# Combining two expert outputs per token: three rooms of 16 tokens, token-wise products, and paired stores

## The chip, the core and the metric

The kernel runs on one core of a Trainium2 chip. The metric is the device time of one execution in microseconds; smaller is better. Before the change the median of three runs is 239.19 us (239.14 to 239.21).

## The reference

There are 16 x 1024 = 16,384 tokens. Each has two expert outputs of 512 float32 numbers and two weights, and the result is their weighted sum:

```python
# expert_outputs (16, 1024, 2, 512), combine_weights (16, 1024, 2), float32
weights = combine_weights[..., np.newaxis]
return np.sum(expert_outputs * weights, axis=2).astype(np.float32)   # (16, 1024, 512)
```

A token brings 4 KB in and 2 KB out. All tokens together bring 67.1 MB in, 33.6 MB out, and 0.13 MB of weights. Nothing is reused.

## The kernel before

The tokens are spread over the 128 partitions, 128 tokens to a partition. In the first region of the tensors each partition owns 120 consecutive tokens, in the second one 8, so that a tile's tokens are one unbroken run of memory in each partition. A tile of 12 tokens is thus loaded as 128 rows of 48 KB and stored as 128 rows of 24 KB. There are ten tiles of 12 tokens and a last one of 8. Tile 0 is loaded in two parts, first 2 tokens (in rows of 4 KB) and then 10.

The loop over the tiles (line 68) takes a buffer from a pool of four (`ipool`, `bufs=4`, 48 KB per partition each, 192 KB in all), issues the load on SP's queue (line 75), computes in place, and issues the store from the same buffer. The results are packed into the lower half of the buffer, `ot`. The load of tile g + 4 needs the buffer of tile g, so on SP it waits until the store of tile g has landed.

For tiles 0 to 8, VectorE (DVE in the profile) does everything in two large instructions: line 84 multiplies both halves of 12 tokens by their weights (128 x 12,288 elements), and line 85 adds the halves (128 x 6,144). ScalarE (ACT) only issues the stores (line 86). For the last two tiles ACT multiplies the first half of each token by its weight (line 92), token after token. For tile 9 DVE multiplies the second half (line 107) and adds (line 108); for the last tile DVE does both for one token in one instruction, `scalar_tensor_tensor`: second half times weight plus first half (line 96). The stores of these two tiles are issued on SP (line 109), behind all loads.

Ahead of the loop, DVE clears a small tile `zt`, which ACT's queue writes to the start of 16 stretches of the output (line 58; the real results overwrite it later); then the weights `wt` are loaded on ACT's queue in two parts (line 62), and a one-element activation (line 66) brings in ACT's table. A tile scheduler sets the order on each engine; within one queue it is as in the text, but for the store of tile 8, which stands between the eighth and the ninth activation of tile 9.

SP and ACT each have one DMA queue. Both are served by the same 16 DMA engines; each engine moves 8 of the 128 rows of a transfer. In the page "q1" is SP's queue and "q10" is ACT's.

Of the kernel before, what the change touches and what calls it, by code (L numbers as in the profile page):

```python
# [1 line left out]

# [4 lines left out]


@with_exitstack
def kernel(  # L10
    ctx: ExitStack,
    tc: tile.TileContext,
    expert_outputs: bass.AP,
    combine_weights: bass.AP,
    out: bass.AP,
):

    nc = tc.nc  # L20
    b, s, k, h = expert_outputs.shape
    assert k == 2
    n = b * s
    P = nc.NUM_PARTITIONS
    per = n // P
    assert per * P == n
    J, LAST = 12, 8
    main = per - LAST
    assert main % J == 0
    eo = expert_outputs.rearrange("b s k h -> (b s) (k h)")  # L30
    cw = combine_weights.rearrange("b s k -> (b s) k")
    o = out.rearrange("b s h -> (b s) h")

    def rows(x):

        a = x[0 : P * main, :].rearrange("(p t) f -> p t f", p=P)
        b = x[P * main : n, :].rearrange("(p t) f -> p t f", p=P)
        return lambda t, c: a[:, t : t + c, :] if t < main else b[:, t - main : t - main + c, :]

    eo, cw, o = rows(eo), rows(cw), rows(o)  # L40

    dt = mybir.dt.float32
    mult = mybir.AluOpType.mult
    add = mybir.AluOpType.add
    copy = mybir.ActivationFunctionType.Copy

    last = main // J

    wpool = ctx.enter_context(tc.tile_pool(name="w", bufs=1))
    ipool = ctx.enter_context(tc.tile_pool(name="in", bufs=4))  # L50

    wt = wpool.tile([P, per * k], dt)


    zt = wpool.tile([16, 128], dt)
    nc.vector.memset(zt, 0.0)  # L56
    first = out.rearrange("b s h -> (b s) h")[0 : P * main, :].rearrange("(q t) h -> q (t h)", q=16)
    ahead = nc.scalar.dma_start(out=first[:, 0:128], in_=zt)  # L58

    with tc.issue_after(ahead.ins):  # L60
        for t, c in ((0, main), (main, LAST)):
            nc.scalar.dma_start(
                out=wt[:, k * t : k * (t + c)].rearrange("p (t k) -> p t k", k=k), in_=cw(t, c)
            )
        warm = wpool.tile([P, 1], dt)
        nc.scalar.activation(out=warm, in_=nc.const_aps.tensor(1.0, (P, 1), dt), func=copy)  # L66

    for g in range(last + 1):
        et = ipool.tile([P, J, k * h], dt)

        ot = et.rearrange("p j f -> p (j f)")[:, 0 : J * h].rearrange("p (j f) -> p j f", f=h)
        t0, c = g * J, J if g < last else LAST

        for a, m in ((0, 2), (2, c - 2)) if g == 0 else ((0, c),):
            nc.sync.dma_start(  # L75
                out=et[:, a : a + m],
                in_=eo(t0 + a, m),
                max_dma_last_dim=k * h * 4 if g + a == 0 else None,
            )
        if g < last - 1:  # L80

            wb = wt[:, g * J * k : (g + 1) * J * k].unsqueeze(2).to_broadcast([P, J * k, h])
            ek = et.rearrange("p j (k h) -> p (j k) h", k=k)
            nc.vector.tensor_tensor(out=ek, in0=ek, in1=wb, op=mult)  # L84
            nc.vector.tensor_tensor(out=ot, in0=et[:, :, 0:h], in1=et[:, :, h : 2 * h], op=add)  # L85
            nc.scalar.dma_start(out=o(t0, c), in_=ot)
            continue


        for i in range(c):  # L90
            t = t0 + i
            nc.scalar.activation(  # L92
                out=et[:, i, 0:h], in_=et[:, i, 0:h], func=copy, scale=wt[:, 2 * t : 2 * t + 1]
            )
            if g == last:
                nc.vector.scalar_tensor_tensor(  # L96
                    out=ot[:, i, :],
                    in0=et[:, i, h : 2 * h],
                    scalar=wt[:, 2 * t + 1 : 2 * t + 2],
                    in1=et[:, i, 0:h],  # L100
                    op0=mult,
                    op1=add,
                )
        if g < last:
            w1 = wt.rearrange("p (t k) -> p t k", k=k)[:, t0 : t0 + c, 1:2]
            x1 = et[:, :, h : 2 * h]
            nc.vector.tensor_tensor(out=x1, in0=x1, in1=w1.to_broadcast([P, c, h]), op=mult)  # L107
            nc.vector.tensor_tensor(out=ot, in0=et[:, :, 0:h], in1=x1, op=add)  # L108
        nc.sync.dma_start(out=o(t0, c), in_=ot[:, 0:c])


# [1 line left out]
_INS = ['expert_outputs', 'combine_weights']  # L113
_OUTS = [((16, 1024, 512), 'float32')]


# [23 lines left out]
```

## Time and profile before

| | before |
|---|---|
| median of three runs | 239.19 us |
| span of the profiled execution | 237.34 us |
| DMA traffic | 100.80 MB in 3,760 packets |
| DVE busy | 194.1 us, 29 instructions |
| ACT busy | 14.0 us, 22 instructions |
| TensorE, GpSimd | no work of the kernel |

The profiled execution has no separately listed time of its own; the span covers the work from the first to the last instruction on the core, and the runs without a profile take 239.19 us, 1.85 us more than the span. The clock of TensorE plays no part, as it has no work.

How to read the page: "busy" is the time in which an engine executed an instruction. A DMA packet here is one row of a transfer (or a 4-byte write that raises a semaphore at its end; 16 for each DMA). "Idle before, releaser" says how long the engine waited ahead of a group of instructions and what ended the longest part of the wait. "Queue's own waits" of SP are the waits of the engine that only issues DMAs.

### The profile page before, as it was taken

The numbers are of one execution on the slowest core, as the hardware profiler recorded it, in microseconds if no ns is written. First come the engines' busy times: TensorE is split into PE (matmuls) and PEld (weight loads), VectorE is DVE, ScalarE is ACT, GpSimd is POOL, SyncE is SP. The second block draws the span as 40 slices with busy tenths as digits, with TensorE's granted clock in tenths as the row PEclk, the third lists the DMA queues.
The fourth block names the chain that finished last, engine by engine and source line by source line (L and its number), as shares of the span: only waits on it lengthen the run. The fifth ranks groups of instructions, "written<-read, shape, count | busy, mean of one in ns | idle before, by whom it ended". The sixth has DMA issues, their size and how long they took to land.

```text
span 237.3 us, 157 instructions
## 1 busy us (share of the span) xinstructions
DVE 194.1 (82%) x29; ACT 14.0 (6%) x22; POOL 0.2 (0%) x4
## 2 busy tenths in 40 slices
DVE  0008999999999999999999889969996998785710
ACT  2000000000000000000000000000000000740800
POOL 0000000000000000000000000000000000000000
DMA  7999999989899999999898999999998979999997
GB/s 289 452 474 398 398 448 480 398 356 505 352 443 435 427 464 464 398 398 530 348 514 348 447 418 443 464 464 398 398 522 348 522 344 451 464 398 442 406 434 309
DMA packets 3760, 100.80 MB, mean 425 GB/s; under 512 B 544, under 2 KB 688, under 8 KB 944
## 3 DMA queue, kind: packets, MB, share of 16 engines
q1 hardware_dynamic: 2144, 72.35, 71.0%
q10 hardware_dynamic: 1616, 28.45, 27.9%
HBM read 67.24 MB, written 33.56 MB: 425 GB/s over the span
## 4 chain that ended last, share of the span: by engine, by line
DMA 59%; DVE 34%; ACT 2%; ACTq 0%; DVEq 0%; issue 0%; SPq 0%
DMA out_dram<-et 29%; DMA et<-in_expert_outputs_dram 23%; DVE et L84 22%; DVE et L85 11%; DMA wt<-in_combine_weights_dram 7%; ACT et L92 2%; DVE et L96 1%; DVEq L135 0%; ACTq L135 0%; ACTq L58 0%; DVE zt L56 0%; DVEq L84 0%; SPq L75 0%; ACTq L92 0%
## 5 line engine op out<-in xcount | busy, mean ns | idle before, releaser
L84 DVE TENSOR_TENSOR et<-et,wt 128x12288 f32<-128x12288 f32 x9 | 116.6, 12955 | 24.1 <-DMA wt<-in_combine_weights_dram 17.5
L85 DVE TENSOR_TENSOR et<-et 128x6144 f32<-128x6144 f32 x9 | 59.0, 6557 | 0.3
L92 ACT ACTIVATE et<-et,wt 128x512 f32<-128x512 f32 x20 | 12.5, 708 | 208.6 <-DMA et<-in_expert_outputs_dram 208.6
L96 DVE SCALAR_TENSOR_TENSOR et<-et,wt 128x512 f32<-128x512 f32 x8 | 5.6, 746 | 3.9 <-ACT et L92 3.6
L107 DVE TENSOR_TENSOR et<-et,wt 128x6144 f32<-128x6144 f32 x1 | 6.6, 6557 | 2.3 <-DMA et<-in_expert_outputs_dram 2.3
L108 DVE TENSOR_TENSOR et<-et 128x6144 f32<-128x6144 f32 x1 | 6.6, 6558 | 0.9 <-ACT et L92 0.9
L66 ACT ACT_TABLE_LOAD x1 | 1.3, 1283 | 2.4 <-issue 2.4
L56 DVE MEMSET zt<- 16x128 f32 x1 | 0.2, 165 | 0.8 <-PEq L124 0.8
L66 ACT ACTIVATE warm<-const-float32-1.0 128x1 f32<-128x1 f32 x1 | 0.2, 202 | 0.0
L124 POOL MEMSET const-bfloat16-1.0<- 128x1 bf16 x1 | 0.1, 102 | 0.0
L124 POOL MEMSET const-uint8-127<- 128x1 uint8 x1 | 0.1, 101 | 0.0
L124 POOL MEMSET const-float32-0.0<- 128x1 f32 x1 | 0.1, 99 | 0.2 <-issue 0.2
L124 POOL MEMSET const-float32-1.0<- 128x1 f32 x1 | 0.1, 98 | 0.0
## 6 DMA issues: line engine op xcount, KB each, us to landing
et<-in_expert_outputs_dram SPq DMA_DIRECT2D x9, 6144.0 KB, 29.9
out_dram<-et ACTq DMA_DIRECT2D x9, 3072.0 KB, 33.0
et<-in_expert_outputs_dram SPq DMA_DIRECT2D x1, 5120.0 KB, 17.0
et<-in_expert_outputs_dram SPq DMA_DIRECT2D x1, 4096.0 KB, 25.1
out_dram<-et SPq DMA_DIRECT2D x1, 3072.0 KB, 14.6
out_dram<-et SPq DMA_DIRECT2D x1, 2048.0 KB, 10.0
et<-in_expert_outputs_dram SPq DMA_DIRECT2D x1, 1024.0 KB, 5.0
wt<-in_combine_weights_dram ACTq DMA_DIRECT2D x1, 120.0 KB, 17.0
```

What stands on the lines that cost most here:

```text
L56: nc.vector.memset(zt, 0.0)
L66: nc.scalar.activation(out=warm, in_=nc.const_aps.tensor(1.0, (P, 1), dt), func=copy)
L84: nc.vector.tensor_tensor(out=ek, in0=ek, in1=wb, op=mult)
L85: nc.vector.tensor_tensor(out=ot, in0=et[:, :, 0:h], in1=et[:, :, h : 2 * h], op=add)
L92: nc.scalar.activation(out=et[:, i, 0:h], in_=et[:, i, 0:h], func=copy, scale=wt[:, 2 * t : 2 * t + 1])
L96: nc.vector.scalar_tensor_tensor(out=ot[:, i, :], in0=et[:, i, h : 2 * h], scalar=wt[:, 2 * t + 1 : 2 * t + 2], in1=et[:, i, 0:h], op0=mul ...
L107: nc.vector.tensor_tensor(out=x1, in0=x1, in1=w1.to_broadcast([P, c, h]), op=mult)
L108: nc.vector.tensor_tensor(out=ot, in0=et[:, :, 0:h], in1=x1, op=add)
L124: nc = _bacc.Bacc("TRN2", target_bir_lowering=False, num_devices=1)
```

## The change

The loop and the pool are replaced by a fixed program in which every instruction is placed by hand (`tc.manual_schedule()`: the order on each engine is the order of the text).

- **Regions.** The first region gives each partition 116 tokens, the second 12.
- **Rooms.** One tile `et` of 48 tokens per partition (192 KB) is divided into three rooms of 16 tokens side by side. Tile g lives in room g modulo 3.
- **Tiles.** Nine tiles of 12, 16, 16, 16, 16, 16, 16, 8 and 12 tokens. Loads are rows of 64 KB (16 tokens), 48 KB (12) and 32 KB (8); tile 0 still comes as 2 and 10 tokens.
- **Products.** `combine` treats every token the way the last tile was treated before: one activation on ACT (line 76) and one `scalar_tensor_tensor` on DVE (line 77). These are 128 instructions on each engine. On DVE the 20 large instructions are gone.
- **Stores.** Seven stores instead of eleven. Tiles 3 and 4 (rooms 0 and 1) and tiles 6 and 7 (rooms 0 and 1) are stored together: the earlier tile packs its results into the upper half of its room (`up`, from its last token backwards), the later one into the lower half of the next room, so that both lie side by side and leave as one row of 64 KB (32 tokens) or 48 KB (24 tokens). The other stores are rows of 24 KB (tile 0, tile 8) and 32 KB (tiles 1, 2, 5).
- **Queues.** Loads on SP. The first five stores are issued on ACT, the last two (tiles 6 and 7; tile 8) on SP. The load of tile g + 3 is issued after the store that holds tile g has landed; for tiles 6 and 7 this is the common store of tiles 3 and 4. On SP the order is: loads 0 to 8, store of tiles 6 and 7, store of tile 8.

```diff
-    J, LAST = 12, 8
-    main = per - LAST
...
+    ROOM, ROOMS = 16, 3
+    TILES = [12, 16, 16, 16, 16, 16, 16, 8, 12]
+    STORES = [[0], [1], [2], [3, 4], [5], [6, 7], [8]]
+    AHEAD = 2
+    main = per - TILES[-1]
+    starts = [sum(TILES[:g]) for g in range(len(TILES))]
...
-    ipool = ctx.enter_context(tc.tile_pool(name="in", bufs=4))
+    et = pool.tile([P, ROOMS * ROOM, k * h], dt)
+    halves = et.rearrange("p j (k h) -> p (j k) h", k=k)
...
+    def load(g):
+        at, c = g % ROOMS * ROOM, TILES[g]
+        for a, m in ((0, AHEAD), (AHEAD, c - AHEAD)) if g == 0 else ((0, c),):
+            nc.sync.dma_start(
+                out=et[:, at + a : at + a + m],
+                in_=eo(starts[g] + a, m),
+                max_dma_last_dim=k * h * 4 if g + a == 0 else None,
+            )
+    def combine(g, up):
+        at, c = g % ROOMS * ROOM, TILES[g]
+        base = k * at + (ROOM if up else 0)
+        for i in range(c - 1, -1, -1) if up else range(c):
+            t = k * (starts[g] + i)
+            x0, x1 = halves[:, k * (at + i), :], halves[:, k * (at + i) + 1, :]
+            nc.scalar.activation(out=x0, in_=x0, func=copy, scale=wt[:, t : t + 1])
+            nc.vector.scalar_tensor_tensor(
+                out=halves[:, base + i, :], in0=x1, scalar=wt[:, t + 1 : t + 2], in1=x0, op0=mult, op1=add
+            )
+        return base
+    with tc.manual_schedule():
...
+        for g in range(ROOMS):
+            load(g)
+        for j, st in enumerate(STORES):
+            bases = [combine(g, up=len(st) == 2 and g == st[0]) for g in st]
+            c = sum(TILES[g] for g in st)
+            q = nc.sync if j >= len(STORES) - 2 else nc.scalar
+            q.dma_start(out=o(starts[st[0]], c), in_=halves[:, bases[0] : bases[0] + c, :])
+            for g in st:
+                if g + ROOMS < len(TILES):
+                    load(g + ROOMS)
...
-    for g in range(last + 1):
-        et = ipool.tile([P, J, k * h], dt)
...
-        if g < last - 1:
-            wb = wt[:, g * J * k : (g + 1) * J * k].unsqueeze(2).to_broadcast([P, J * k, h])
-            nc.vector.tensor_tensor(out=ek, in0=ek, in1=wb, op=mult)
-            nc.vector.tensor_tensor(out=ot, in0=et[:, :, 0:h], in1=et[:, :, h : 2 * h], op=add)
-            nc.scalar.dma_start(out=o(t0, c), in_=ot)
```

The line numbers 64, 76, 77 and 100 of the kernel after are its loads, its activations, its DVE instructions and its stores.

More of the change, by code (lines that the diff above doesn't have):

```diff
@@ L26 @@
     assert per * P == n
-    J, LAST = 12, 8
-    main = per - LAST
[L29 to L32, printed above, removed]
-    def rows(x):
[L36 to L40, printed above, removed]
+    ROOM, ROOMS = 16, 3
+    TILES = [12, 16, 16, 16, 16, 16, 16, 8, 12]
+    STORES = [[0], [1], [2], [3, 4], [5], [6, 7], [8]]
+    AHEAD = 2
+    assert sum(TILES) == per and [g for st in STORES for g in st] == list(range(len(TILES)))
+    main = per - TILES[-1]
+    starts = [sum(TILES[:g]) for g in range(len(TILES))]
+    def rows(x):
+        first = x[0 : P * main, :].rearrange("(p t) f -> p t f", p=P)
+        second = x[P * main : n, :].rearrange("(p t) f -> p t f", p=P)
+        return lambda t, c: first[:, t : t + c, :] if t < main else second[:, t - main : t - main + c, :]
+    flat = out.rearrange("b s h -> (b s) h")
+    eo = rows(expert_outputs.rearrange("b s k h -> (b s) (k h)"))
+    cw = rows(combine_weights.rearrange("b s k -> (b s) k"))
+    o = rows(flat)
     dt = mybir.dt.float32
@@ L45 @@
     copy = mybir.ActivationFunctionType.Copy
-    last = main // J
-    wpool = ctx.enter_context(tc.tile_pool(name="w", bufs=1))
-    ipool = ctx.enter_context(tc.tile_pool(name="in", bufs=4))
[L52 to L61, printed above, removed]
+    pool = ctx.enter_context(tc.tile_pool(name="all", bufs=1))
+    et = pool.tile([P, ROOMS * ROOM, k * h], dt)
+    halves = et.rearrange("p j (k h) -> p (j k) h", k=k)
+    wt = pool.tile([P, per * k], dt)
+    zt = pool.tile([16, 128], dt)
+    warm = pool.tile([P, 1], dt)
+    def load(g):
[18 more added lines that the diff above has]
+    with tc.manual_schedule():
+        nc.vector.memset(zt, 0.0)
+        ahead = flat[0 : P * main, :].rearrange("(q t) h -> q (t h)", q=16)
+        nc.scalar.dma_start(out=ahead[:, 0:128], in_=zt)
+        for t, c in ((0, main), (main, per - main)):
             nc.scalar.dma_start(
@@ L64 @@
             )
-        warm = wpool.tile([P, 1], dt)
         nc.scalar.activation(out=warm, in_=nc.const_aps.tensor(1.0, (P, 1), dt), func=copy)
-    for g in range(last + 1):
-        et = ipool.tile([P, J, k * h], dt)
[L71 to L79, printed above, removed]
-        if g < last - 1:
-            wb = wt[:, g * J * k : (g + 1) * J * k].unsqueeze(2).to_broadcast([P, J * k, h])
-            ek = et.rearrange("p j (k h) -> p (j k) h", k=k)
-            nc.vector.tensor_tensor(out=ek, in0=ek, in1=wb, op=mult)
-            nc.vector.tensor_tensor(out=ot, in0=et[:, :, 0:h], in1=et[:, :, h : 2 * h], op=add)
-            nc.scalar.dma_start(out=o(t0, c), in_=ot)
[L87 to L109, printed above, removed]
@@ new lines @@
+        for g in range(ROOMS):
[3 more added lines that the diff above has]
+            c = sum(TILES[g] for g in st)
+            assert bases[-1] == bases[0] + sum(TILES[g] for g in st[:-1])
+            q = nc.sync if j >= len(STORES) - 2 else nc.scalar
[3 more added lines that the diff above has]
+                    load(g + ROOMS)
```

## Prediction

> **What bounds the kernel now.** I read the page's shares first, then its DMA parts, then the DMA share by stretches, then the waits of SP's queue and the chain that ended last.
>
> ```profile
> DVE 194.1 (82%) x29; ACT 14.0 (6%) x22; POOL 0.2 (0%) x4
> ...
> DMA packets 3760, 100.80 MB, mean 425 GB/s; under 512 B 544, under 2 KB 688, under 8 KB 944
> ...
> q1 hardware_dynamic: 2144, 72.35, 71.0%
> q10 hardware_dynamic: 1616, 28.45, 27.9%
> ...
> L84 DVE TENSOR_TENSOR et<-et,wt 128x12288 f32<-128x12288 f32 x9 | 116.6, 12955 | 24.1 <-DMA wt<-in_combine_weights_dram 17.5
> L85 DVE TENSOR_TENSOR et<-et 128x6144 f32<-128x6144 f32 x9 | 59.0, 6557 | 0.3
> L92 ACT ACTIVATE et<-et,wt 128x512 f32<-128x512 f32 x20 | 12.5, 708 | 208.6 <-DMA et<-in_expert_outputs_dram 208.6
> L96 DVE SCALAR_TENSOR_TENSOR et<-et,wt 128x512 f32<-128x512 f32 x8 | 5.6, 746 | 3.9 <-ACT et L92 3.6
> ```
>
> DVE looks like the limit at 82%, but the two queues took 71.0 + 27.9 = 98.9% of the DMA engines' time: 234.7 of 237.3 us. The stretches (their columns: start:end, length, busy time of DVE, ACT and GpSimd, TensorE's clock, DMA share, GB/s) say where the rest is:
>
> ```profile
> 2.00:40.00 38.00, 21.51 (x3) 1.49 (x2) 0.00 (x0) 1.00 1.03 437
> 40.00:120.00 80.00, 79.83 (x9) 0.00 (x0) 0.00 (x0) 1.00 1.00 428
> 120.00:200.00 80.00, 73.28 (x8) 0.00 (x0) 0.00 (x0) 1.00 1.01 437
> ...
> 2.00:236.00 234.00, 193.97 (x28) 13.96 (x22) 0.00 (x0) 1.00 1.00 431
> ```
>
> A packet is credited to the stretch in which it starts, so single stretches stray around 1.00. From 2 to 236 us the share is 1.00: no engine of the 16 ever ran dry. By the packet records the first row starts at 1.8 us and the last ends at 236.1. So 234.3 us is the DMA's own work and 3.0 us its head and tail. The waits of SP's queue and the chain agree:
>
> ```profile
> SPq L75 <- DMA out_dram<-et: 174.1, 7, 45.8
> ```
> ```profile
> 76.96 30.61 DMA out_dram<-et
> 107.57 0.02 SPq L75
> 107.59 0.04 issue
> 107.63 29.93 DMA et<-in_expert_outputs_dram
> 137.56 0.03 issue
> ```
>
> SP waits 174.1 us for stores to free buffers, and the chain goes from store to load to DVE. Yet these waits cost nothing, because other transfers filled the engines meanwhile. DVE's 194 us lie beneath the DMA. The kernel gets faster only through less DMA work, and slower as soon as the queues run dry.
>
> **The bytes, and the packets.** The bytes stay at 100.7 MB plus completion writes. What changes is the number of rows. Median durations in the trace's packet records: 16 KB 611 ns, 24 KB 912, 32 KB 1,213, 40 KB 1,514, 48 KB 1,815, 4-byte completion 9. Every 8 KB costs 301 ns; 9 ns are left over whatever the size. A 64 KB row doesn't occur before; continued, it costs 8 x 301 + 9 = 2,417 ns.
>
> Each engine moves 8 rows of a transfer (16 of the first load's 4 KB rows). Loads before: 16 + 8 + 9 x 8 + 8 = 104 rows; after: 16 + 8 + 6 x 8 + 8 + 8 = 88. Stores before: 11 x 8 = 88; after: 7 x 8 = 56. That is 48 fewer. DMAs go from 26 to 20: 6 fewer completion writes. 54 x 9 ns = 0.49 us saved on each engine, all on the path, since the engines are never idle.
>
> Here the Trainium skill can be weighed. The page "DMA: Bandwidth & Descriptors", section "Anatomy of one DMA", puts about 2.0 us of fixed cost on each DMA; six fewer would by that estimate save 12 us. The share of 1.00 across DMA boundaries says that this cost lies under other transfers. The same page, under "Where 436 GB/s comes from", says that HBM, at about 358 GB/s per core, binds transfers between HBM and SBUF; fewer rows would then gain nothing. Here 431 GB/s passed, so the trace speaks against it.
>
> **The products.** DVE loses 20 large instructions (116.6 + 59.0 us, and 13.1 for lines 107 and 108) and gets 128 of 746 ns; ACT gets 128 of 708 ns. In the last tile eight tokens took 5.78 us on DVE by the timeline, 0.72 each. DVE falls to about 92 us and ACT to 128 x 0.61 = 78. None of this is on the path; it only matters how soon a tile's store is issued: 0.8 us for the first activation plus 16 x 0.72, or 12.3 us (before: 19.5 for 12 tokens). ACT's store stands behind its activations and waits for DVE's last product, and the next tile's activations queue behind it; that tile is usually still loading. Some 200 more instructions must be fetched; the trace has 0.02 to 0.05 us between instructions and no fetch stall, so I take 0, with 0 to 0.6 us as bounds (0.6 is twice the 301 ns of 8 KB on one engine).
>
> **Three rooms instead of four.** This is where time can be lost: a load waits for a store of the tile three back, two tiles share one store, and SP's queue is in order. Behind load 6, which waits for the common store of 3 and 4, stand loads 7 and 8 and both last stores. The rows show how queues share: each engine takes one row from each queue in turn. About 1.1 us pass from issue to first row (0.72 to 1.8), and from a store's last row to the release of SP about 1.6 us (fitted: stepping before's rows through with these two numbers puts loads 4 to 10 at 63.9, 85.8, 107.6 ... 194.8; the trace has 64.1, 85.9, 107.6 ... 194.7).
>
> Counting back from the end, if no gap occurs: the last row ends at 236.1 - 0.5 = 235.6. Store 8 (8 x 0.912) starts at 228.3; store 6+7 (8 x 1.815) at 213.8; load 8 (14.5) at 199.3, which is load 7's end. Load 7 (9.7), load 6 (19.3) and store 5 (9.7) fill 160.6 to 199.3; load 5 and store 3+4 (19.3 each) fill 121.9 to 160.6. Against this, what must be issued in time:
> - Load 5 at about 117 + 1.1 (store 2: eight turns of 2.417 + 1.213 from 86, plus 1.6). Needed at 121.9: cover near 4 us.
> - Store 5: load 5 lands near 144, tile 5 to 156.3, first row 157.4. Needed at 160.6, when store 3+4 runs out and load 6 has not been released: cover 3.2.
> - Store 6+7: load 6 lands at 191.2 (199.3 - 9.7 + 1.6), 12.3 + 0.8 + 5.8 of products to 210.1, first row 211.2. Needed at 213.8: cover 2.6.
> - Store 8: load 8 lands at 215.4, products to 224.8, first row 225.9. Needed at 228.3: cover 2.4.
>
> All four hold, so I price the gaps at 0, with the bound above in the rival. Head and tail stay: load 0 and the weights come as before, and the last store's completion too. One more term: the 48 KB rows that ran between 41 and 47 us, as the first store began, took up to 2.33 us instead of 1.815, together 0.6 us per engine. It happens once, at the first store, which remains; I keep it, with 0 to twice its size as bounds.
>
> **Sum.** 237.34 - 0.49 = 236.85 us of span; with the 1.85 us that lie around it, 238.70 us. With the 0.6 us either way: 238.1 to 239.3. A change below 0.2% (0.48 us) can't be told from none by a measurement of this kernel; the forecast sits just beyond it.
>
> **Rivals.**
> - *The 64 KB rows are split into two of 32 KB.* For: no row above 48 KB occurs in the trace. Against: 48 KB rows go unsplit. Price: 6 x 8 loads and 8 stores more, 56 x 9 ns = 0.50 us, which eats the gain: 239.2.
> - *Queues run dry at the end* (slower). Place: load 8's last row, after which only store 6+7 can follow. It decides at 24 tokens x pace: a cover of 2.6 us is used up when a token takes 0.83 us instead of 0.72. For: the first three DVE products of the last tile started 0.85 us apart; at 0.85 all along, 24 x 0.02 = 0.5 us would be lost: 239.2. At 0.95 it is 2.9 us: 241.6. Against: the later ones started 0.67 apart while transfers ran at full rate. Where it decides I take a pace of 0.88, 240.0.
> - *The first-store stall grows*, or fetching shows: up to 0.6 us on top, 239.3.
>
> **Chances.** Forecast (saving holds, no gap) 65%: it spreads over 238.1 to 239.0 and is beyond the 0.2% in two of three cases (0.43 faster, 0.22 same). Split rows 8%, nearly all within 0.2%. Dry queues 20%, nearly all slower. Stall or fetch 7%, half within 0.2% and half slower. Together: faster 0.44, same 0.32, slower 0.24. The range: 238.2 below; above, it takes in the dry queue up to 240.4, a pace of about 0.90. The likeliest case's own range is 238.1 to 239.0.
>
> **What would show it.** Right: 2,896 packets (16 engines x (88 + 56 + 17 + 20)), 64 KB rows at 2.42 us, DMA share 1.00 from 2 to 235, span near 236.9, DVE near 95 us. Wrong: a stretch with share clearly below 1 near 121, 160, 213 or 228 us (dry queues: read which store came late); more packets than 3,000 (split rows); DVE products further apart than 0.8 us.

## The result, and the profile after

The kernel after takes 242.36 us (median of 4 runs, 242.19 to 242.72) against 239.20 us for the kernel before on the same chip: a ratio of 1.0135, 95% interval 1.0121 to 1.015. It is 3.2 us slower; the forecast was 0.5 us less. Its profiled span is 240.41 us, 3.07 us more than before.

From the page of the kernel after:

```profile
DVE 87.3 (36%) x129; ACT 80.8 (34%) x130; POOL 0.2 (0%) x4
...
DMA packets 2899, 100.83 MB, mean 419 GB/s; under 512 B 448, under 2 KB 592, under 8 KB 848
...
q1 hardware_dynamic: 1856, 76.55, 74.9%
q10 hardware_dynamic: 1040, 24.26, 23.7%
q14 instruction: 3, 0.02, 0.0%
...
L77 DVE SCALAR_TENSOR_TENSOR et<-et,wt 128x512 f32<-128x512 f32 x128 | 87.1, 745 | 138.6 <-ACT et L76 136.8
L76 ACT ACTIVATE et<-et,wt 128x512 f32<-128x512 f32 x128 | 79.3, 707 | 141.8 <-DMA et<-in_expert_outputs_dram 127.5
```

DVE has fallen from 194 to 87 us, and the packets from 3,760 to 2,896 and three that did not exist before: queue 14 fetches instructions during the run. The two data queues still took 98.6% of the engines' time, but of a longer span. So the engines were as busy as before, with fewer rows and the same bytes. They must have worked more slowly somewhere, and the stretches show where (start:end, length, busy DVE, ACT and GpSimd, clock, DMA share, GB/s):

```profile
63.00:66.00 3.00, 0.75 (x1) 1.54 (x3) 0.00 (x0) 1.00 0.89 382
66.00:69.00 3.00, 2.83 (x5) 3.00 (x6) 0.00 (x0) 1.00 1.22 492
69.00:72.00 3.00, 3.00 (x5) 3.00 (x6) 0.00 (x0) 1.00 1.13 350
...
160.00:170.00 10.00, 0.48 (x1) 0.00 (x0) 0.00 (x0) 1.00 0.99 370
165.00:170.00 5.00, 0.00 (x0) 0.00 (x0) 0.00 (x0) 1.00 1.22 413
```

Share and GB/s are both credited to the stretch in which a packet starts, so their quotient is the rate of busy engines, nearly free of that straying. It is 382 / 0.89 = 429 in the first line, and 433 in the undisturbed stretches before. From 66 to 69 it is 403, from 69 to 72 it is 310, from 165 to 170 it is 339. In the last line the engines were busy for 1.22 x 5 = 6.1 us and moved what takes 413 x 5 / 433 = 4.8 us at the full rate: 1.3 us were lost while the share said "full". In the packet records these are a few rows of each engine: usually 1.213 us for 32 KB and 2.418 for 64 KB, near 68 and 167 us up to 2.1 and 3.9 us, on all 16 engines within some 3 us. The chain and SP's waits tell what else happened there:

```profile
SPq L64 <- DMA out_dram<-et: 164.5, 5, 46.6
```
```profile
76.32 40.52 DMA out_dram<-et
116.84 0.02 SPq L64
116.86 0.04 issue
116.90 31.66 DMA et<-in_expert_outputs_dram
...
160.51 24.89 DMA out_dram<-et
185.42 0.03 SPq L64
185.45 0.03 issue
185.47 32.02 DMA et<-in_expert_outputs_dram
```

Load 3 was issued at 64.7 us and load 6 at 163.1 us, each after the load before it had landed (64.4 and 148.6). SP's queue was empty for about 6 us the first time and for about 20 the second, with only stores running. Both slow spots lie where loads begin again. I call this a restart.

The packet records account for the 3.07 us of span. On one engine a row begins 3 to 4 ns before the record of the row ahead of it ends, so a row saved is worth 9 less 3.5, or 5.5 ns. "Excess" is what rows took beyond their usual durations, summed over all rows and divided by 16 engines, apart for the rows that start before and after 6 us; "late" is the end of the last row less that of the eighth last:

| us | before | after | difference |
|---|---|---|---|
| rows and completions saved (54 per engine x 5.5 ns) | | | -0.30 |
| excess before 6 us | 0.57 | 0.41 | -0.16 |
| excess after 6 us | 0.54 | 3.31 | +2.77 |
| late last engine | 0.18 | 0.71 | +0.53 |
| last row's end to the span's end | 1.20 | 1.43 | +0.23 |
| sum | | | +3.07 |

Further down, "the excess" is that after 6 us. This is the account of one execution of each kernel.

### The profile page after: what moved, and what is told of

It is laid out like the page before. It is cut to its first block, busy times and chain, and to the rows that moved or that the text cites. A ratio compares the mean times of both kernels' runs of the same rounds, so it can differ in the third digit from the quotient of the medians.

```text
span 240.4 us, 413 instructions
## 1 busy us (share of the span) xinstructions
DVE 87.3 (36%) x129; ACT 80.8 (34%) x130; POOL 0.2 (0%) x4
## 4 chain that ended last, share of the span: by engine, by line
DMA 69%; DVE 10%; ACT 7%; another core or an unknown queue 6%; issue 1%; ACTq 0%; SPq 0%; DVEq 0%
DMA et<-in_expert_outputs_dram 41%; DMA out_dram<-et 27%; DVE et L77 10%; ACT et L76 7%; SPq L64 0%; DVEq L129 0%; ACTq L129 0%; ACTq L100 0%; ACTq L76 0%
## 5 line engine op out<-in xcount | busy, mean ns | idle before, releaser
L77 DVE SCALAR_TENSOR_TENSOR et<-et,wt 128x512 f32<-128x512 f32 x128 | 87.1, 745 | 138.6 <-ACT et L76 136.8
L76 ACT ACTIVATE et<-et,wt 128x512 f32<-128x512 f32 x128 | 79.3, 707 | 141.8 <-DMA et<-in_expert_outputs_dram 127.5
```

The source lines that it names most:

```text
L76: nc.scalar.activation(out=x0, in_=x0, func=copy, scale=wt[:, t : t + 1])
L77: nc.vector.scalar_tensor_tensor(out=halves[:, base + i, :], in0=x1, scalar=wt[:, t + 1 : t + 2], in1=x0, op0=mult, op1=add)
```

## The experiments

Times are medians, with the ratio to the kernel before measured beside them; rows, stalls and excess are those of the one profiled execution of each run. Theory R (later G): restarts of a queue beside the other cost time. F: instruction fetches in the run. S: 64 KB rows. P: token-wise products.

**e1_solo34: load 6 released by a single store.**

```diff
-    STORES = [[0], [1], [2], [3, 4], [5], [6, 7], [8]]
+    STORES = [[0], [1], [2], [3], [4], [5], [6, 7], [8]]
```

> The changed kernel with tiles 3 and 4 stored each on its own (rows of 32 KB, one more DMA); tiles 6 and 7 stay paired. Theory R (a queue that ran empty and starts again beside the other one stalls the engines' rows: here SP's load queue, empty from 63 to 69 us and from 144 to 168 us in the kernel after, each restart costing about 1.2 us): load 6 is released by store 3 before load 5 ends, the rows near 166 to 170 us go back to 2.42 and 1.21 us, 1.2 us less than after: about 241.1. Rival S (64 KB rows are slower whenever they alternate with stores): nothing moves, 242.4. Rival F (instruction fetches inside the run): nothing moves, 242.4.

241.77 us, ratio 1.011 (1.0097 to 1.0123). The second slow spot is gone:

```profile
165.00:170.00 5.00, 5.00 (x8) 3.18 (x6) 0.00 (x0) 1.00 1.18 511
```

511 / 1.18 = 433, the full rate, with 64 KB and 32 KB rows taking turns. The excess fell from 3.31 to 1.80 us. The median fell by only 0.6 us, not by the 1.2 expected; in the profiled execution one engine ended 1.2 us behind the eighth last (238.23 against 237.03). R is right about the stall; S falls, since 64 KB rows ran beside stores from 75 to 185 us at their usual 2.418 us.

**e2_wt2_sp and e3_both: store 0 freed from the weights.**

```diff
-        for t, c in ((0, main), (main, per - main)):
-            nc.scalar.dma_start(...)
+        def weights(q, t, c):
+            q.dma_start(...)
+        weights(nc.scalar, 0, main)
...
         for g in range(ROOMS):
             load(g)
+        weights(nc.sync, main, per - main)
```

> The changed kernel with the second part of the weights (12 tokens, 8 rows per engine of 96 bytes) loaded on SP's queue after load 2 instead of on ACT's. In the kernel after these rows took turns with 64 KB rows until 36.9 us, and store 0, issued at 27.4, stood behind them. Theory R: store 0 lands some 5 to 8 us earlier, load 3 is released at about 58 to 60 us, near the end of load 2 (63); if it makes it, the stall at 67 to 70 us goes and the time falls by 1.2 us to 241.1; if the queue still runs empty for a moment, the stall stays and 242.4 with it. Rivals S and F: 242.4.

> Both edits, tiles 3 and 4 stored alone and the second part of the weights on SP. Theory R: no restart of the load queue, 2.4 us less than after: 239.9, with 64 KB rows of 2.42 us throughout. Rivals S and F: 242.4.

e2: 242.39 us, 1.0133 (1.012 to 1.0146). e3: 242.3 us, 1.0123 (1.01 to 1.0146), with single runs from 240.76 to 242.73. Store 0 landed at 57.4 instead of 64.6 us, load 3 was issued at 57.5, and the stall at 67 to 70 us disappeared in both. But others came: 0.6 us near 30 and 36 as store 0 began (0.5 before), and 0.5 us near 83 to 85. There it was ACT's queue that had run empty: store 1 landed at about 75, store 2 was issued at 80.2. In e2 the stall at 166 to 169 stayed (1.6 us), in e3 another 0.6 us appeared near 212. The excess was 2.98 and 1.87 us. In e2 a stall was moved, not saved. In e3 the excess is 1.4 us below that of the kernel after, but the last engine ended 1.8 us behind the eighth last (238.97 against 237.15), and the time stayed. The expected 1.2 and 2.4 us did not come.

**e4_12x4: the sizes of before with token-wise products.**

```diff
-    ROOM, ROOMS = 16, 3
-    TILES = [12, 16, 16, 16, 16, 16, 16, 8, 12]
-    STORES = [[0], [1], [2], [3, 4], [5], [6, 7], [8]]
+    ROOM, ROOMS = 12, 4
+    TILES = [12] * 10 + [8]
+    STORES = [[g] for g in range(11)]
```

> The changed kernel's program (token-wise products, manual order) with the sizes of before: four rooms of 12 tokens, tiles of ten times 12 and one of 8, each stored alone, the last two on SP. No 64 KB rows, no pairs, and a load queue that never runs empty. Theory R: as before but for fetches, 239.2 to 239.8. Rival S: 239.2 too. Rival F, or the products themselves being the cause: stays near 242.

242.43 us, 1.0139 (1.0126 to 1.0152). R's 239.2 to 239.8 was missed, but not through stalls: the excess is 0.70 us (0.54 in the kernel before). The time went into idle engines at the end:

```profile
231.00:234.00 3.00, 2.48 (x4) 0.95 (x2) 0.00 (x0) 1.00 0.04 16
```

With quick products the first stores are issued earlier (27.5 us instead of 38.0 for store 0), stores take turns with loads throughout, and push the loads back: the last load was issued at 187.4 us instead of 194.7 and landed at 227.0 instead of 219.8. When its products were under way, no store was left to run. That DVE's slow products held stores back in the kernel before, and that these covered the end, is my reading of the two traces; no run tests it by itself.

**e7_12x4_pair89: the same with a long store under the last products.** `STORES` ends in `[8, 9], [10]`.

> Four rooms of 12 tokens as in e4_12x4, but tiles 8 and 9 stored together on SP (48 KB rows), so that a long store lies under the products of the last tile. The load queue never runs empty, and the gap of about 3 us at 231 to 234 us should close. Theory R: no stall but the one at the first store, and only the fetches remain: 239.3 to 239.9. If the token-wise products or the manual order cost something of their own: above 240.5.

241.69 us, 1.0107 (1.0094 to 1.012). The excess is again 0.70 us, and the gap moved:

```profile
216.00:219.00 3.00, 2.25 (x4) 0.53 (x1) 0.00 (x0) 1.00 0.03 14
```

About 2.5 us of idle engines, as the paired store was issued only at 218.3 us, when the rows of the last load had run out on nearly all engines (it landed at 219.0). Less that gap the time is 239.2. So the expected 239.3 to 239.9 was missed through idle time that I had not seen; in e4 and e7 token-wise products came with no stretched rows beyond those at the first store.

**e5_12x3_pair34: restarts without 64 KB rows.** `ROOM, ROOMS = 12, 3`, tiles as in e4, only tiles 3 and 4 paired.

> The changed kernel's program with rows no longer than 48 KB: three rooms of 12 tokens, ten tiles of 12 and one of 8, only tiles 3 and 4 stored together (48 KB rows). The load queue must run empty before load 3 (three rooms) and before load 6 (waits for the common store). Theory R (restart of an empty queue beside the other): rows around both restarts are stretched, about three quarters of the 1.2 us that 64 KB and 32 KB rows showed, 0.9 us each, so the rows' excess over their usual durations is about 0.6 + 1.8 = 2.4 us per engine. Rival S (only 64 KB rows are slow): excess 0.6 us, as in the kernel before. Both leave the gap of about 3 us at the end that four rooms of 12 showed (231 to 234 us), so 242 under S and 244 under R.

243.40 us, 1.0179 (1.0154 to 1.0205), single runs from 242.37 to 245.3. Rows of 48 and 24 KB stall as well, 1.1 us at the restart of load 6 near 135 us (0.9 expected):

```profile
134.00:137.00 3.00, 0.00 (x0) 0.00 (x0) 0.00 (x0) 1.00 1.26 401
```

401 / 1.26 = 318. There is more at 59 to 70, 111, 163 to 165 and 203 to 206 us. The excess of 3.86 us is above the expected 2.4; it is that of the slowest of the six runs. S is out.

**e6_before_more_instr: instruction fetches alone.**

```diff
         nc.scalar.activation(out=warm, in_=nc.const_aps.tensor(1.0, (P, 1), dt), func=copy)
+        for _ in range(108):
+            nc.scalar.activation(out=warm, in_=nc.const_aps.tensor(1.0, (P, 1), dt), func=copy)
+        fill = wpool.tile([P, 1], dt)
+        for _ in range(128):
+            nc.vector.memset(fill, 0.0)
```

> The kernel before with 108 one-element activations on ACT and 128 one-element memsets on DVE put in while both are idle ahead of tile 0, so that both engines have about as many instructions as in the kernel after. Nothing else moves. Theory F (instruction fetches of 8 KB inside the run hold up the engine that serves them by 0.3 us and a stretched row, and the last row of that engine ends the kernel): three fetches, one or two engines end 0.4 to 0.9 us behind the rest, 239.5 to 240.0. Rival (fetches cost nothing): 239.1.

240.43 us, 1.0056 (1.0044 to 1.0068): 1.3 us more, from instructions that lie in idle time. From its DMA view and its last stretches:

```profile
q14 instruction: 2, 0.02, 0.0%
```
```profile
235.00:236.00 1.00, 0.00 (x0) 0.00 (x0) 0.00 (x0) 1.00 0.77 328
236.00:237.00 1.00, 0.00 (x0) 0.00 (x0) 0.00 (x0) 1.00 0.04 16
237.00:238.00 1.00, 0.00 (x0) 0.00 (x0) 0.00 (x0) 1.00 0.04 16
```

Two fetches of 8 KB, 0.31 us each, and the data rows beside them took up to 0.6 us longer. Fifteen engines are done by 236.4 us; one is still busy with its last two rows of 16 KB and ends at 237.6. A share of 0.04 is one engine of 16 for 0.6 us, and the kernel waits for it. Its rows can be followed back, each from the end of the one ahead of it: at 11.24 us this engine served one of the two fetches, and the 40 KB row behind it took 2.11 us instead of 1.51; smaller stretches followed. The last engine of the kernel after had served a fetch too, at 223.7 us, with a row of 2.23 us instead of 1.82 behind it. F holds, and costs more than the 0.4 to 0.9 us expected. In e4, e5 and e7, which have three fetches each, the engines stood idle for 2.5 to 3.2 us near the end, and there the last one ended within 0.11 us of the eighth last.

A late engine also occurs without a fetch: 3 of 21 runs of the kernel before, taken beside e8, lasted 240.1 to 240.3 us, and in e8's profiled execution (240.12 us) one engine ended 0.9 us behind the next with no fetch in the trace. But in e6 all five runs lay from 240.28 to 240.62.

**e8_before_swap78 and its control e9_before_rooms: one restart in the kernel before.**

```diff
+    rooms = ipool.tile([P, 4 * J, k * h], dt)
...
-        et = ipool.tile([P, J, k * h], dt)
+        et = rooms[:, ROOM[g] * J : (ROOM[g] + 1) * J]   # ROOM = [0, 1, 2, 3, 0, 1, 2, 0, 3, 1, 2]; control: 0 to 3 in turn
```

> The kernel before with its four buffers as one tile of four rooms, and tiles 7 and 8 with their rooms exchanged: load 7 goes to the room of tile 4 instead of tile 3, load 8 to that of tile 3. Instructions, rows and bytes stay. Load 7 now waits for store 4 instead of store 3, some 10 us past the end of load 6 (137 us), so SP's queue is empty from about 137 to 148 us while stores run on, and then starts again. Theory R: the rows around the restart are stretched, 0.7 to 1.0 us per engine more than before, 239.8 to 240.2; if the stores give out before load 7 starts, up to 1.5 us of idle engines come on top and can be told apart, since the DMA share falls below 1 there. Rival (an empty load queue costs nothing as long as stores run, as the prediction had it): 239.1, or the idle time alone.

> The control for e8_before_swap78: the kernel before with its four buffers as one tile of four rooms, used in the old order. Every theory: 239.1.

e9: 239.13 us, 0.9995 (0.9986 to 1.0004). e8: 239.25 us, 1.0004 (0.9987 to 1.0021). SP's queue did run empty: load 7 was issued at 143.2 us, its first rows came at 146.8, and from about 138 to 146 only store rows ran. But nothing was stretched there (0.03 us):

```profile
146.00:149.00 3.00, 3.00 (x1) 0.00 (x0) 0.00 (x0) 1.00 1.11 475
```

475 / 1.11 = 428. The kernel after holds a second such case: ACT's queue had no rows from 114.1 to 139.8 us, then store 3+4 began beside load 5, and no row was stretched. This speaks against R as I had put it: a restart need not cost anything. Hence the next three, which ask whether the stalls belong to the pattern of the transfers (G) or to the token-wise products and their instructions (P).

**e10_after_one_add: the kernel after without its products.**

```diff
-        for i in range(c - 1, -1, -1) if up else range(c):
...
-            nc.scalar.activation(out=x0, in_=x0, func=copy, scale=wt[:, t : t + 1])
-            nc.vector.scalar_tensor_tensor(...)
+        x = halves[:, k * at : k * (at + c), :]
+        nc.vector.tensor_tensor(out=halves[:, base : base + c, :], in0=x[:, 0:c, :], in1=x[:, c : 2 * c, :], op=add)
```

> The changed kernel with its DMAs, tiles, rooms and pairs, but without the products: one DVE addition per tile (8.7 us for 16 tokens instead of 11.1) takes the place of the activations and the token-wise products, so the output is not the weighted sum. ACT then only issues stores, and both engines have a dozen instructions: no fetch in the run. Theory G (the stalls come from the pattern of loads and stores): stalls of 1.2 us where load 3 and load 6 restart, as in the kernel after; only the late engine at the end is gone, 241.3 to 241.8. Theory P (they come from the token-wise products or the longer instruction stream): no stall but the first store's, 238.7, which is the time that the prediction gave.

240.93 us, 1.0084 (1.0053 to 1.0115), single runs from 240.20 to 242.91.

```profile
69.00:72.00 3.00, 3.00 (x1) 0.00 (x0) 0.00 (x0) 1.00 1.11 350
...
165.00:170.00 5.00, 0.00 (x0) 0.00 (x0) 0.00 (x0) 1.00 1.03 419
```

The first restart stalls as in the kernel after (350 / 1.11 = 315); the second lost 0.3 us instead of 1.35 (419 / 1.03 = 407). No fetch, and the last row ended 0.55 us behind the eighth last. The time is below the 241.3 to 241.8 expected under G. G holds and P falls: the stall comes without a single token-wise instruction. How much it costs varies: 0.3 or 1.35 us for the same restart in the two traces, and the runs lie 2.7 us apart.

**e11_12x4_swap78: the exchange of rooms in e4.** `PLACE = [0, 1, 2, 3, 0, 1, 2, 0, 3, 1, 2]` in place of `g % ROOMS`.

> Four rooms of 12 tokens with token-wise products (e4_12x4) and the exchange of the rooms of tiles 7 and 8 (e8_before_swap78): the load queue runs empty once, before load 7, in a kernel whose rows and stores are those of before. Theory P: a stall of 0.7 to 1 us at that restart, since the products are token-wise, 243.2. Theory G: no stall there, as in e8_before_swap78, 242.4, the gap of 3 us at the end included.

244.13 us, 1.0212 (1.0198 to 1.0225). Inconclusive on its question: in the changed kernel's text load 7 stands ahead of the products of tile 4, so in the shared room these waited for load 7 and worked on its data. The order was another than planned. It did have idle engines at 178 to 179 us and 1.4 us of stretched rows right behind them, at 183 to 186.

**e12_before_bufs3: many restarts in the kernel before.**

```diff
-    ipool = ctx.enter_context(tc.tile_pool(name="in", bufs=4))
+    ipool = ctx.enter_context(tc.tile_pool(name="in", bufs=3))
```

> The kernel before with three buffers instead of four: the load queue runs empty before load 3 and before several later loads, with 48 KB and 24 KB rows and DVE's large products. Idle engines are expected too (about 2.4 us near 53 and 77 us, when both queues are empty), seen as a DMA share below 1. Theory G: rows around the restarts are stretched, 1 us or more beyond the first store's 0.6; 245. Theory P: no stretched rows, only idle time; 243 to 244.

249.42 us, 1.0423 (1.0391 to 1.0455). Two of its restarts:

```profile
127.00:130.00 3.00, 3.00 (x1) 0.00 (x0) 0.00 (x0) 1.00 1.42 401
...
172.00:175.00 3.00, 3.00 (x1) 0.00 (x0) 0.00 (x0) 1.00 1.41 393
```

401 / 1.42 = 282 and 393 / 1.41 = 279, the lowest of the rates shown here, in a kernel with DVE's large products, no pair, no fetch and no row above 48 KB. The stalls near 56 to 60, 128, 173 and 214 to 219 us cost 1.2 to 1.7 us each; the excess is 6.91 us, and 2.9 us of idle engines come on top. Other restarts of the same run cost nothing to speak of: load 4 at 84 us, stores at 101 and 147 us, 0.03 us or less each. G holds; the time is well above the 245 expected.

**e13_smooth_one_add and e14_smooth: a load queue without long breaks.** The edits of e3, and tiles chosen so that store 0 comes early; e13 has the single addition of e10, e14 the real products.

```diff
-    TILES = [12, 16, 16, 16, 16, 16, 16, 8, 12]
+    TILES = [8, 12, 16, 16, 16, 16, 16, 16, 12]
```

> Three rooms of 16 tokens, 64 KB rows, but arranged so that no queue should run empty beside the other: tiles of 8, 12, six times 16 and 12 tokens, so that store 0 is issued early; all stores single but 6 and 7; the second part of the weights on SP. One DVE addition per tile instead of the products, as in e10_after_one_add (the output is not the weighted sum), so no fetch in the run. Theory G: only the first store's stall of 0.6 us is left and the rows saved show: 238.7 to 239.0. If 64 KB rows or three rooms cost something by themselves: 240 or more.

> The same arrangement with the real token-wise products on ACT and DVE. Theory G with F: as e13_smooth_one_add plus the late engines of three instruction fetches, 0.6 to 1.3 us: 239.3 to 240.2. Without F: the same time as e13_smooth_one_add.

e13: 239.83 us, 1.0035 (1.0021 to 1.0048). e14: 241.23 us, 1.0092 (1.0078 to 1.0106). The restarts of the load queue are gone. ACT's queue still had no rows from 60.0 to 69.2 us in e13, and beginning again cost 0.1 us, all that e13 lost behind 30 us. But as store 0 began, 1.0 us went into stretched rows (0.5 in the kernel before), so e13 missed 238.7 to 239.0 by 0.8 us: the excess was 1.10 us and ate the saving. e14 has an excess of 1.02, three fetches, a last engine 1.5 us behind the eighth last (238.33 against 236.82) and 0.6 us of idle engines at 209 us; it lies 1.0 us above the 239.3 to 240.2 expected. No version beat the kernel before.

Four of the runs, put side by side, divide the loss in another way than the account of the one execution. Their medians, in us:

| | load restarts as in the kernel after | load queue without long breaks |
|---|---|---|
| token-wise products, three fetches | 242.36 (after) | 241.23 (e14) |
| one addition per tile, no fetch | 240.93 (e10) | 239.83 (e13) |

The products with their fetches are worth 1.4 us in either column, the arrangement 1.1 us in either row, and e13 is still 0.7 us above the kernel before. The arrangement differs in more than the restarts (order of the tiles, single stores, second part of the weights on SP), and e10's runs scatter by 2.7 us, so these are rough shares.

## Why the prediction was wrong

**Bound, rows and bytes: right, but for the size of the saving.** The DMA engines set the time, and no row was split. 64 KB rows take 2.418 us (2.417 predicted), and there are 2,896 packets besides the fetches. The saving per row was put too high: 9 ns is what is left of the row's own record, but the records overlap by 3 to 4 ns, so that 54 rows less are worth 0.30 us, not 0.49. No run measured this saving by itself. The 2.0 us per DMA that the prediction weighs come from a section on DMAs issued by GpSimd; here SP and ACT issue them, so its 12 us were not an estimate for this kernel.

**Products: right.** DVE has 87 us (92 predicted, and 95 at the prediction's end), 0.69 us per token, and all four covers held: store 6+7 was issued at 210.9 us (first row expected at 211.2, so issue at 210.1) and store 8 at 226.7, both before the queue ahead of them ended. Store 5 held only just: load 5 landed at 148.6 us instead of 144, so the store was issued at 160.5, 1.0 us before the first engine was through with store 3+4, where the prediction had a cover of 3.2 us behind its 1.1 from issue to first row. No gap as in the rival "queues run dry". e4, e7 and e14 show that this rival was real: 0.6 to 3.2 us, where tiles were cut less fortunately.

**"All four hold, so I price the gaps at 0": the step that failed.** The sum asked only whether some engine would stand idle. It had load 6 waiting for the common store until 160.6 us and took this as free, since store rows filled the engines. They did, but where loads came back, rows were stretched: +2.77 us of excess in all, about 2.7 of it at two restarts. e1 took one away and its stall went; e10 and e12 showed such stalls without token-wise products, and e5 and e12 without 64 KB rows. What was shown is that the stalls sit where loads or stores begin again after a while without them (e3's near 212 us too: these rows are the last loads ahead of the first store since 196 us), and that such a beginning cost from nothing to 1.7 us. What stretches the rows, and what decides the size, is open: e8, the kernel after at 139.8 us and e12 had restarts that cost nothing, and e3, e5, e10 and e12 scatter by 2 to 3 us from run to run, while before, e4 and e9 scatter by 0.3 at most but for single runs. The trace of before held a warning, in the 0.54 us lost once, as the first store began beside the loads; I priced it as a singular event, not as the price of such a beginning.

**Load 3, overlooked.** The covers treat loads 5 to 8; load 3 was not stepped through. Its restart came from the second part of the weights: 8 rows of 96 bytes per engine, each taking turns with a 64 KB row, held ACT's queue until 36.9 us, and store 0, issued at 27.4, stood behind them and landed at 64.6. e2 moved these rows to SP's queue, and the stall at load 3 went. The DMA view of the kernel before had shown that little load with 31.1 us to landing; below it, the line of the kernel after:

```profile
wt<-in_combine_weights_dram ACTq DMA_DIRECT2D x1, 8.0 KB, 31.1
```
```profile
wt<-in_combine_weights_dram ACTq DMA_DIRECT2D x1, 12.0 KB, 35.6
```

A queue position is not free because the transfer is small. The section "Issuing engines are not separate DMA queues" of the Trainium skill's page "DMA: Bandwidth & Descriptors" says that transfers of different engines run interleaved on the same 16 engines; the rows agree: those 8 rows took from 19.5 to 36.9 us, one 64 KB row of 2.42 us between each two, so that a turn here is one row, however long.

**Fetches: bound too low, the second step that failed.** I took 0 and allowed 0.6 us. In e6 more instructions alone cost 1.3 us (1.05 to 1.63 by the interval), and in the kernel after the last engine is 0.53 us later than before; between the rows of the table of four, products and fetches together make 1.4 us. The reasoning looked at the engine that waits for instructions, and there nothing shows. The cost falls on a DMA engine: a fetch and the row beside it make one of 16 late, and in a kernel that keeps all 16 full to the end nothing lets it catch up. The Trainium skill ("Runtime: NRT & Kernel Launch", "Instruction fetch mechanics") calls the cost of crossing into the next block of instructions mostly hidden. For the engine that runs the instructions the trace agrees: the 16 products on DVE that began at 65.2 us, with a fetch at 74.75, took 11.07 us like those at 38.1. For the time of a DMA-bound kernel e6's 1.3 us do not.

**The range.** Its upper end of 240.4 came from the rival of a dry end; the other costs stood there with 0.6 us each and 7% together. In the profiled execution they were worth 2.8 and about 0.5 us; by the table of four, roughly 1.1 us for the arrangement, 1.4 for products and fetches, and 0.7 beside.

## What to carry to other kernels

In a kernel that is bound by DMA, look at how long each queue is empty, not only at whether engines idle: DMA share can read 0.99 while 370 GB/s pass instead of 433, as from 160 to 170 us here, and GB/s divided by share shows it. A break in the load or the store stream may cost nothing or, here, up to 1.7 us; keep both going side by side, and step through every queue in order, small transfers included. Instructions are not free there either: 236 more in e6 brought two fetches onto the DMA engines, and the slowest of 16 set the time.

## What the runs showed of the hardware beyond that

- Stalls at restarts hit the 16 engines within some 3 us of each other (near 168 us in the kernel after, 134 in e5): first the last row of the running stream, then the first row of the returning one; nearly all later rows are at their usual durations.
- Quick products can cost time at the end: in e4 the last load landed 7.2 us later than in the kernel before, with the same bytes and a DVE less than half as busy.
- The usual row durations are very regular: 301 ns for each 8 KB and 9 ns per row, from 4-byte completions to 64 KB rows; the medians of every run agree within 7 ns. The next row on the engine begins 3 to 4 ns before the record ends.
